# Retention heads 1 to 3: values and gate in seven quarter products, weighted values by tokens

## The chip, the cores and the metric

The kernel runs on one core of one Trainium2 chip. The metric is the device time of one execution in microseconds (us); lower is better. TensorE multiplies, VectorE and ScalarE do the element work, GpSimd (POOL) some of it, and SyncE (SP) issues the loads.

## What is computed

A trunk of two layers over 512 tokens of width 1024, all in float32: retention, FFN, RG-LRU, FFN, with norms before and after each. The change is in the retention layer:

```python
proj = x @ w_in                      # x: normed, 512 x 1024
q, k, v, g = jnp.split(proj, ...)    # 4 heads: q, k 256 wide, v, g 512 wide
q = rope(q); k = rope(k) * (DK ** -0.5)
scores = (q @ k.T) * decay           # causal, decay by head
o = scores @ v                       # the reference does it in chunks of 128
oc = o - o.mean(-1)
o = oc * lax.rsqrt(mean(oc * oc) + EPS)
return (o * silu(g)) @ w_out
```

## The kernel before

**Products.** Every float32 operand is split into a high part in fp32r (a cast on ScalarE, L163) and the rest as a low part (a subtraction on VectorE, L165). A product is then a triple, `mm3` (L291 to L293): high by high, high by low, low by high, three matmuls into the same PSUM bank. `Pre` makes the parts of the normed input (the norm's factor for a token is multiplied in later: `pre0.cols` holds it by tokens, `pre0.rb` spread over partitions).

**Heads.** The loop over four heads stands in `trunk` behind `rope`. For a head it forms the values by tokens (`pv`, four token tiles, weights in four chunks), centers them (`center`), then the queries and keys by features (`group`, two tiles each) with their rotation, the first half of the gate (`gate(0)`), the scores in four tiles that keep only the causal columns (512, 384, 256, 256 wide), `gate(1)`, and the weighted values by features: for each of four feature tiles the four score tiles are taken through (L291 to L293, `pav`). As tokens then lie along the free axis, the norm over a head's 512 features needs TensorE twice: `rchain` sums the squares with a vector of ones (L364, `st_gn`), takes the root in small instructions on VectorE (L374 to L381), and spreads it with diagonal matrices (L394, `rb_gn`). The products of the gate with the norm's factor and the `Silu` stand at L771 and L773. The results are split again (`Hr`) for the output projection `ro`, in four groups of two tiles over 16 tiles of features.

**FFN.** The FFN's up projection is made by blocks already: `Corners` holds four quarters of the normed input (token half by odd or even feature tile) and four sums of them, `Form` makes the sums of weight quarters `t1` to `t4` (L187), and seven products stand for eight. `LEFT`, `WEIGHTS` and `LATER_PAIR` name which sum meets which, `turn` (L860) transposes the results.

**What sets the order.** Each engine runs its instructions in the order written, which a planner lays out: `later` keeps a clock that `mm3` moves on by 0.4224 ns a column (`NS_PER_COL`), and a step given to `later.after(ns, ...)` is written when that clock is due. `later.until(cond)` writes waiting steps at once until the condition holds. `order` lists the weight items; `advance` splits items ahead of their use (five of the plain ones, 12 us of products of the `Form` ones, eight at most held), and `load_ahead` issues loads four ahead on SP. SBUF is a pool of 50 slots of 128x1024 (`SLOTS`), PSUM has six banks for sums (`acc`) and two others (`aux`).

## Time and profile before

| | us |
|---|---|
| median of 3 runs | 1385.68 (1385.38 to 1386.33) |
| profiled execution | 1384.3 |
| its span, first to last instruction | 1382.4 |
| TensorE busy in it | 1346.6 |
| VectorE busy in it | 900.6 |
| ScalarE busy in it | 665.4 |

The profile lists one execution, engine by engine. A busy time of TensorE counts any moment with a matmul in flight; matmuls overlap, so how long one takes in a row of them is read from the distance of their starts. The first product of head 1 starts at 86.65 us, heads 2 and 3 follow 78.8 us apart, and the output projection starts behind head 3.

### The profile page before, as it was taken

How to read it: one execution, taken by the hardware profiler on the slowest of the kernel's cores; microseconds unless marked ns; L12 is line 12 of the kernel's file. 1: busy time of each engine (PE TensorE's matmuls, PEld its weight loads, DVE VectorE, ACT ScalarE, POOL GpSimd, SP SyncE). 2: the span in 40 equal slices, each digit the busy share in tenths (PEclk: the TensorE clock that was granted, in tenths of full speed). 3: DMA queues.
4: the chain of work that ended last, by engine and by line, in shares of the span. 5: the costliest groups of instructions: out<-in, count | busy, mean ns of one | idle time of the engine just before them, and what ended most of it. 6: DMA issues, size and time to landing. Idle time of an engine off the chain costs nothing.

```text
span 1382.4 us, 17330 instructions
## 1 busy us (share of the span) xinstructions
PE 1346.6 (97%) x6760; PEld 1144.8 (83%) x6760; DVE 900.6 (65%) x1320; ACT 665.4 (48%) x983; POOL 117.6 (9%) x129
## 2 busy tenths in 40 slices
PE   8999999999999899999999999999997999999996
PEld 6888888888897678888889998888986888888886
DVE  7755455567337988787521787788579987775313
ACT  5423333334435665546422537787465555564311
POOL 1000000000015300000000710000052000000001
PEclk9999999999999999999999999999999999999998
DMA  8232312223343223233432543224333233323311
GB/s 332 76 102 62 115 63 85 77 76 112 102 141 119 93 92 94 89 122 101 119 100 78 169 136 105 78 77 153 122 108 121 78 106 122 113 89 103 92 61 62
DMA packets 48914, 146.77 MB, mean 106 GB/s; under 512 B 5472, under 2 KB 13792, under 8 KB 48832
## 3 DMA queue, kind: packets, MB, share of 16 engines
q1 hardware_dynamic: 45072, 135.16, 30.0%
q0 software_dynamic: 2608, 9.45, 2.0%
q8 instruction: 53, 0.87, 0.3%
q10 hardware_dynamic: 1152, 1.05, 0.2%
q14 instruction: 29, 0.24, 0.1%
HBM read 137.25 MB, written 8.39 MB: 105 GB/s over the span
## 4 chain that ended last, share of the span: by engine, by line
PE 54%; DVE 3%; POOL 1%; issue 1%; ACT 1%; DMA 0%; POOLq 0%; ACTq 0%; DVEq 0%
PE ps_fo L291 6%; PE ps_fo L292 6%; PE ps_fo L293 6%; PE b L291 3%; PE b L293 3%; PE b L292 3%; PE c L291 2%; PE c L293 2%; PE c L292 2%; PE a L292 2%; PE a L293 2%; PE a L291 2%; PE ps_y L291 1%; PE ps_y L293 1%; PE ps_y L292 1%; PE ps_lo L291 1%
## 5 line engine op out<-in xcount | busy, mean ns | idle before, releaser
L291 PE MATMUL ps_fo<-hh,wh_fo 128*128 128x512 f32 (+1 forms) x440 | 153.2, 348 | 0.0
L292 PE MATMUL ps_fo<-hl,wh_fo 128*128 128x512 f32 (+1 forms) x440 | 152.5, 347 | 0.0
L293 PE MATMUL ps_fo<-hh,wl_fo 128*128 128x512 f32 (+1 forms) x440 | 152.5, 347 | 0.0
L165 DVE TENSOR_TENSOR wl_s_t<-t,wh_s_t 128x1024 fp32r<-128x1024 f32 x80 | 98.0, 1248 | 21.7 <-ACT wh_s_t L163 21.7
L165 DVE TENSOR_TENSOR wl_s_b<-wr,wh_s_b 128x1024 fp32r<-128x1024 f32 x60 | 74.1, 1238 | 32.1 <-ACT wh_s_b L163 32.1
L291 PEld LDWEIGHTS ps_fo<-hh,wh_fo 128*128 128x128 f32 x440 | 83.3, 189 | 10.3
L293 PEld LDWEIGHTS ps_fo<-hh,wl_fo 128*128 128x128 f32 x440 | 83.3, 189 | 10.3
L292 PEld LDWEIGHTS ps_fo<-hl,wh_fo 128*128 128x128 f32 x440 | 83.3, 189 | 10.2
L163 ACT CAST wh_s_t<-t 128x1024 fp32r<-128x1024 f32 x80 | 80.6, 1051 | 15.9 <-DVE t L187 15.6
L163 ACT CAST wh_s_b<-wr 128x1024 fp32r<-128x1024 f32 x60 | 61.0, 1061 | 3.3 <-DVE wl_s_t L165 3.3
L861 ACT COPY hf<-turn 128x512 f32<-128x512 f32 x40 | 21.5, 590 | 79.6 <-PE turn L860 79.6
L165 DVE TENSOR_TENSOR wl_fo<-wr,wh_fo 128x1024 fp32r<-128x1024 f32 (+1 forms) x48 | 51.8, 1131 | 7.9 <-ACT wh_fo L163 7.9
L187 DVE TENSOR_TENSOR t<-wr,wr 128x1024 f32<-128x1024 f32 x40 | 50.4, 1260 | 0.0
L187 DVE TENSOR_TENSOR t<-t,wr 128x1024 f32<-128x1024 f32 x40 | 48.8, 1220 | 0.2
L163 ACT CAST wh_fo<-wr 128x1024 fp32r<-128x1024 f32 (+1 forms) x48 | 43.9, 984 | 0.0
L165 DVE TENSOR_TENSOR wl_g<-wr,wh_g 128x1024 fp32r<-128x1024 f32 x16 | 19.5, 1223 | 35.0 <-ACT wh_g L163 34.9
L431 POOL TENSOR_TENSOR pssq_f<-pssq_f,psq_f 128x256 f32<-128x256 f32 x28 | 35.7, 1285 | 35.1 <-ACT psq_f L430 34.2
L773 ACT ACTIVATE sg<-sg 128x512 f32<-128x512 f32 x16 | 10.1, 632 | 58.9 <-DVE sg L771 58.9
L771 DVE TENSOR_TENSOR sg<-ps_g,rb_r 128x512 f32<-128x512 f32 x16 | 11.1, 692 | 41.3 <-PE ps_g L293 41.3
L291 PE MATMUL b<-wh_s_t,Xf_s3h 128*128 128x512 f32 x80 | 32.2, 403 | 5.7 <-ACT u L956 5.7
L752 ACT ACTIVATE vs<-pv,y_prer 128x512 f32<-128x512 f32 x16 | 11.0, 690 | 53.7 <-PE pv L293 53.7
L293 PE MATMUL c<-wh_s_t,Xf_s1l 128*128 128x512 f32 x80 | 31.9, 399 | 4.4 <-DVE Xf_s1l L492 4.4
(1222 smaller groups left out, 4047.0 us busy)
## 6 DMA issues: line engine op xcount, KB each, us to landing
wr<-in_w_s SPq DMA_DIRECT2D x80, 512.0 KB, 3.9
wr<-in_w_fo SPq DMA_DIRECT2D x40, 512.0 KB, 3.6
wr<-in_w_li SPq DMA_DIRECT2D x24, 512.0 KB, 4.1
wr<-in_w_g SPq DMA_DIRECT2D x16, 512.0 KB, 4.0
wr<-in_w_ro SPq DMA_DIRECT2D x16, 512.0 KB, 3.8
wr<-in_w_v SPq DMA_DIRECT2D x13, 512.0 KB, 3.9
wr<-in_w_lo SPq DMA_DIRECT2D x12, 512.0 KB, 3.8
wr<-in_w_q SPq DMA_DIRECT2D x8, 512.0 KB, 3.7
```

Source lines behind the costliest of these rows:

```text
L163: act.copy(hi[:, :c], raw[:, :c])
L165: dve.tensor_tensor(lo[:, :c], raw[:, :c], hi[:, :c].bitcast(F32), op=ALU.subtract)
L187: dve.tensor_tensor(q[f, e], x, y, op=ALU.add)
L291: pe.matmul(out, lhsT=lh, rhs=rh, start=bool(first), stop=False, skip_group_check=chained)
L292: pe.matmul(out, lhsT=lh, rhs=rl, start=False, stop=False, skip_group_check=chained)
L293: pe.matmul(out, lhsT=ll, rhs=rh, start=False, stop=bool(last), skip_group_check=chained)
L431: eng.tensor_tensor(self.ssq[:, a:b], self.ssq[:, a:b], sq[:, a:b], op=ALU.add)
L752: act.activation(vs[i], pv[i], AF.Copy, scale=pre0.cols[i], accum_out=sm[:, i:i + 1])
L771: dve.tensor_tensor(gr, ps, rb, op=ALU.mult)
L773: later.after(700 * (m + 1), lambda gr=gr: act.activation(gr, gr, AF.Silu))
L861: act.copy(put(m), ps.rearrange("p (m t) -> p m t", m=2))
```

## The change

Head 0 keeps its values and gate as full products, but both now by tokens (`flat`). In heads 1 to 3 values and gate are one product of the normed input with a 1024 by 1024 matrix, made as in the FFN from quarters: rows are token halves, the inner halves are even and odd feature tiles, columns are values and gate. `Whole` forms the four sums of input quarters once, in head 0; `pair_planner` plans the 14 weight items of a head; `head_pair` runs the seven products p1, p5, p2, p6, p3, p7, p4 in six banks and writes the scores between p7 and p4 (`inner`). The weighted values are formed by tokens (`attend`), from score tiles as the fixed operand and values as the moving one, and only for the causal tiles; their square is summed by ScalarE's accumulator (`accum_out`), the root is taken by `root` straight from it, gate and root are multiplied in by VectorE, and the result is transposed in four groups of four (`finish_head`, `turned`). `attend` of a head is written behind the next head's queries; that of head 3 by `later.after(W_AV, ...)` inside the output projection. The diff's core (`root`, `center`, `scores` and `product` hold code that was inline before; `plan_ffn` and the FFN call the shared functions and do the same as before):

```diff
+W_GN_H = 6500
+W_TURN_H = 1500
+W_AV = 4500
+W_HR0 = 0
+W_HR = 1000
...
+    def root(sums, n, name, quick=False):
...
+        return y
...
-            m = sp.tile([P, 4], F32, tag="m", name=f"m_{name}_{a}")[:, :nt]
...
+            y = root(ps[:, :nt], n, f"{name}_{a}", quick)
...
+    LEFT = {"p1": (0, 0), "p2": (0, 1), "p3": "s4", "p4": (1, 1), "p5": "s1", "p6": "s2", "p7": "s3"}
+    class Whole(Pre):
+        def __init__(self, gi, name):
+            super().__init__(gi, name)
+            self.forms = {}
+        def sums(self, xs):
+            full = [[slot(f"X{self.name}f{c}{q}") for c in range(2)] for q in range(2)]
+            s = {f: slot(f"X{self.name}_{f}") for f in ("s1", "s2")}
+            def whole(j):
+                act.activation(full[j % 2][j // 4][:, j % 4 // 2 * S:][:, :S], xs[j], AF.Copy, scale=ng[:, self.gi, j:j + 1])
+            def add(f, x, y, op):
+                if f not in s:
+                    s[f] = slot(f"X{self.name}_{f}")
+                for c in range(2):
+                    dve.tensor_tensor(view(s[f][:, c * S:(c + 1) * S]), part(x, c), part(y, c), op=op)
+            def view(z):
+                return z.rearrange("p (i t) -> p i t", i=2)
+            def part(x, c):
+                if isinstance(x, str):
+                    return view(s[x][:, c * S:(c + 1) * S])
+                return view(full[x[1]][c])[:, :, x[0] * 256:(x[0] + 1) * 256]
+            def two(f):
+                hi, lo = slot(f"X{self.name}_{f}h", F32R), slot(f"X{self.name}_{f}l", F32R)
+                act.copy(hi, s[f])
+                def low():
+                    dve.tensor_tensor(lo, s[f], hi.bitcast(F32), op=ALU.subtract)
+                    self.forms[f] = hi, lo
+                later.after(1500, low)
+            steps = []
+            for j in range(KD):
+                steps += [lambda j=j: whole(j), 1500]
+            by = {z[0]: z for z in Corners.SUMS}
+            for f in ("s1", "s2", "s4", "s3"):
+                steps += [lambda f=f: add(*by[f]), 2500, lambda f=f: two(f), 2500]
+            later.seq(*steps[:-1])
+        def left(self, q, i, p):
+            if isinstance(q, tuple):
+                at = q[0] * 256 + p * P
+                return [z[:, at:at + P] for z in self.tiles[2 * i + q[1]]]
+            later.until(lambda: q in self.forms)
+            return [z[:, i * 256 + p * P:][:, :P] for z in self.forms[q]]
+    def product(key, r, banks, first, pre, done=None):
+        for e in range(2):
+            with Chunk("s", *key, WEIGHTS[r], e) as w:
+                for p in range(2):
+                    for i in range(2):
+                        x = pre.left(LEFT[r], 2 * e + i, p)
+                        mm3(banks[p], x, [z[:, i * S:(i + 1) * S] for z in w], first and not e + i, e + i == 2, True)
+                    if e and done:
+                        done(p)
...
+    HEAD_PAIR = ("p1", "p5", "p2", "p6", "p3", "p7", "p4")
+    head_form = pair_planner("v", t["w_vg"], 0)
+    for h in range(HEADS):
+        if not h:
+            plan_flat("v0", [t["w_v"][:, 2 * c:2 * c + 2].rearrange("p k m -> p (k m)") for c in range(4)])
+        plan(f"q{h}", t["w_q"][h], KD)
+        plan(f"k{h}", t["w_k"][h], KD)
+        if not h:
+            plan_flat("g0", [t["w_g"][:, 2 * c:2 * c + 2].rearrange("p k m -> p (k m)") for c in range(4)])
+        else:
+            for r in HEAD_PAIR:
+                for e in range(2):
+                    head_form(h, r, e)
...
-    pre0 = Pre(0, "r")
+    pre0 = Whole(0, "r")
...
+    def center(h, at, ps, V, apart=False):
+        n = len(ps)
+        vs = [big(f"vs{h}_{at + i}", kind="vs") for i in range(n)]
+        sm = sp.tile([P, 4], F32, tag="sm", name=f"sm{h}_{at}")[:, :n]
+        nm = sp.tile([P, 4], F32, tag="nm", name=f"nm{h}_{at}")[:, :n]
+        vh = []
...
+        def fill(i):
+            act.activation(vs[i], ps[i], AF.Copy, scale=pre0.cols[at + i], accum_out=sm[:, i:i + 1])
+        def finish():
+            later.seq(lambda: None, 700 * n, mean, 1500, low)
+        if apart:
+            return fill, finish
+        for i in range(n):
+            fill(i)
+        finish()
...
+    def head_pair(h, V, sg, inner):
+        A, C, B = ([acc(f"{z}v{h}_{p}") for p in range(2)] for z in "acb")
+        u, five = ([big(f"{z}{h}_{p}", kind=z) for p in range(2)] for z in ("u2v", "p5v"))
+        def silu(g, i):
+            sg[i] = g
+            later.after(800, lambda: act.activation(g, g, AF.Silu, scale=pre0.cols[i]))
+        def seed(p):
+            act.copy(B[p], A[p])
+        def p6(p):
+            act.copy(u[p], B[p])
+        def p5(p):
+            act.copy(five[p], C[p])
+        def p3(p):
+            dve.tensor_tensor(u[p], C[p], u[p], op=ALU.subtract)
+            silu(u[p], p)
+        def p7(p):
+            dve.tensor_tensor(five[p], five[p], B[p], op=ALU.subtract)
+            silu(five[p], 2 + p)
+        fill, finish = center(h, 2, B, V, True)
+        for r, banks, first, done in (("p1", A, True, seed), ("p5", C, True, p5), ("p2", A, False, None), ("p6", B, False, p6),
+                                      ("p3", C, False, p3), ("p7", B, False, p7), ("p4", B, False, fill)):
+            if r == "p4":
+                inner()
+            product(("v", h), r, banks, first, pre0, done)
+            if r == "p2":
+                later.after(100, lambda: center(h, 0, A, V))
+        finish()
+    def finish_head(h, ps, sg, ssq):
+        og = [big(f"og{h}_{i}", kind="og") for i in range(4)]
+        def scaled():
+            y = root(ssq, 512, f"gn{h}")
             for i in range(4):
+                dve.scalar_tensor_tensor(out=og[i], in0=ps[i], scalar=y[:, i:i + 1], in1=sg[i], op0=ALU.mult, op1=ALU.mult)
+        def turned(m):
+            pt = aux(f"turn_r{h}_{m}")
+            for i in range(4):
+                pe.transpose(pt[:, i * P:(i + 1) * P], og[i][:, m * P:(m + 1) * P], ident)
+            hr = big(f"hr{h}_{m}", kind="hr")
+            act.copy(hr, pt)
+            if h < HEADS - 1:
+                raw[4 * h + m] = hr
+            else:
+                split(hr, f"Hr{4 * h + m}", lambda z: Hr.__setitem__(4 * h + m, z))
+            if m < 3:
+                later.after(W_TURN_H, lambda: turned(m + 1))
+        later.seq(lambda: None, 1000, scaled, W_GN_H, lambda: turned(0))
...
+    def attend(h, V, Sc, sg):
+        ssq = sp.tile([P, 4], F32, tag="os", name=f"os{h}")
+        po = []
+        for i in range(4):
+            later.until(lambda: None not in V[:i + 1] + Sc[:i + 1])
+            po.append(acc(f"pav{h}_{i}"))
+            for kk in range(i + 1):
+                hi, lo, q0, _ = Sc[kk]
+                at = i * P - q0
+                mm3(po[i], (hi[:, at:at + P], lo[:, at:at + P]), V[kk], kk == 0, kk == i)
+            sq = big(f"osq{h}_{i}", kind="osq")
+            act.activation(sq, po[i], AF.Square, accum_out=ssq[:, i:i + 1])
+        finish_head(h, po, sg, ssq)
+    decs, before = [dec0], None
+    for h in range(HEADS):
+        if h:
+            decs.append(slot(f"dec_{h}")[:, :640])
+            pool.dma_start(decs[h], t["decay"][h])
+        q, k, V, sg, Sc = [None, None], [None, None], [None] * 4, [None] * 4, [None] * 4
+        if not h:
+            pv = flat("v0")
+        psq = group(f"q{h}", X)
+        if not h:
+            later.until(lambda: pre0.scaled)
+            center(0, 0, pv, V)
+            dve.tensor_tensor(cosr, cos_raw, pre0.rb, op=ALU.mult)
+            dve.tensor_tensor(sinr, sin_raw, pre0.rb, op=ALU.mult)
+            pre0.sums(x0)
+        rope(psq, f"q{h}", q.__setitem__)
+        if h:
+            attend(*before)
+        rope(group(f"k{h}", X), f"k{h}", k.__setitem__)
+        if h:
+            def inner():
+                scores(h, q, k, Sc)
+                if h == HEADS - 1:
+                    for i in range(12):
+                        later.after(W_HR0 + W_HR * i, lambda i=i: split(raw[i], f"Hr{i}", lambda z: Hr.__setitem__(i, z)))
+            head_pair(h, V, sg, inner)
+        else:
+            gate0 = lambda i, ps: act.activation(sg[i], ps, AF.Silu, scale=pre0.cols[i])
+            sg = [big(f"sg0_{i}", kind="sg") for i in range(4)]
+            flat("g0", gate0)
+            scores(0, q, k, Sc)
+        before = h, V, Sc, sg
+    later.after(W_AV, lambda: attend(*before))
...
+    vg = wi[:, 2048:].reshape(2, 2, 2, P, 2, HEADS, 512).transpose(5, 2, 4, 0, 3, 1, 6)
...
-        "w_v": _tiles(wi[:, 2048:4096], 4),
-        "w_g": _tiles(wi[:, 4096:], 8),
+        "w_v": _tiles(wi[:, 2048:2560], 1)[0],
+        "w_g": _tiles(wi[:, 4096:4608], 1)[0],
+        "w_vg": vg.reshape(HEADS * 8, P, 1024),
```

## Rows read from the trace of the kernel before

**Rows 1.** Page: busy times, a costly group, a load (last number: us to landing).

```profile
PE 1346.6 (97%) x6760; PEld 1144.8 (83%) x6760; DVE 900.6 (65%) x1320; ACT 665.4 (48%) x983; POOL 117.6 (9%) x129
...
L861 ACT COPY hf<-turn 128x512 f32<-128x512 f32 x40 | 21.5, 590 | 79.6 <-PE turn L860 79.6
...
wr<-in_w_s SPq DMA_DIRECT2D x80, 512.0 KB, 3.9
```

**Rows 2.** Stretches: busy us of PE, PEld, DVE, ACT, POOL; clock; DMA; GB/s.

```profile
20.00:400.00 380.00, 380.00 (x1838) 322.14 (x1837) 213.29 (x354) 138.03 (x208) 3.63 (x5) 1.00 0.29 96
86.65:165.42 78.77, 78.77 (x378) 66.68 (x377) 42.96 (x74) 26.16 (x40) 0.54 (x1) 1.00 0.26 85
440.00:500.00 60.00, 52.41 (x229) 41.89 (x228) 58.65 (x78) 33.50 (x49) 14.94 (x10) 0.97 0.29 105
500.00:680.00 180.00, 179.36 (x829) 148.84 (x828) 135.67 (x153) 100.70 (x131) 0.00 (x0) 1.00 0.34 106
```

**Rows 3.** Waits of TensorE, whole span: us in total, times, longest.

```profile
PE b L291 <- ACT u L956: 5.7, 1, 5.7
PE c L293 <- DVE Xf_s1l L492: 4.4, 2, 2.5
```

**Rows 4.** Timeline of TensorE, output projection: start us, us, engine, line.

```profile
339.70 0.39 PE L293 MATMUL ps_ro<-Hr10h,wl_ro 128*128 128x512 f32 x1
...
345.82 0.39 PE L293 MATMUL ps_ro<-Hr15h,wl_ro 128*128 128x512 f32 x1
```

**Rows 5.** Timeline of TensorE, weighted values of head 0 and what follows.

```profile
78.94 0.39 PE L291 MATMUL pav<-s_0h,v_0h 128*128 128x512 f32 x1
...
86.65 0.39 PE L291 MATMUL pv<-wh_v,Xr_0h 128*128 128x512 f32 x1
```

**Rows 6.** Timeline of TensorE around the two norm groups of head 0.

```profile
89.85 0.39 PE L293 MATMUL pv<-wh_v,Xr_0h 128*128 128x512 f32 x1
90.08 0.95 PE L364 MATMUL st_gn<-ones_sq,ossq 128*128 128x1 f32 x8
...
91.21 0.40 PE L292 MATMUL pv<-wl_v,Xr_1h 128*128 128x512 f32 x1
...
94.20 0.39 PE L293 MATMUL pv<-wh_v,Xr_3h 128*128 128x512 f32 x1
...
95.56 0.39 PE L292 MATMUL pv<-wl_v,Xr_2h 128*128 128x512 f32 x1
```

**Rows 7.** Timeline of TensorE around four transposes, first FFN.

```profile
505.36 0.39 PE L293 MATMUL a<-wh_s_b,Xf_01l 128*128 128x512 f32 x1
505.59 0.60 PE L860 MATMUL turn<-ident,hr 128*128 128x128 f32 x4
...
506.26 0.40 PE L292 MATMUL a<-wl_s_b,Xf_01h 128*128 128x512 f32 x1
```

**Rows 8.** One tile, 500 to 680 us: ns min/median/max, first, last.

```profile
L860 PE MATMUL turn<-ident,h x40: 270/272/329, 500.6 to 662.5; 128*128 128x128 f32 x40
```

**Rows 9.** Groups of VectorE in head 1's period: busy us, mean ns.

```profile
L165 DVE TENSOR_TENSOR wl_g<-wr,wh_g 128x1024 fp32r<-128x1024 f32 x4 | 4.9, 1223 | 10.9 <-ACT wh_g L163 10.9
...
L771 DVE TENSOR_TENSOR sg<-ps_g,rb_r 128x512 f32<-128x512 f32 x4 | 2.8, 692 | 10.3 <-PE ps_g L293 10.3
...
L748 DVE SCALAR_TENSOR_TENSOR v_0l<-vs,nm,v_0h 128x512 fp32r<-128x512 f32 x2 | 1.4, 747 | 0.9 <-ACT v_0h L743 0.9
```

**Rows 10.** Groups of VectorE, 500 to 680 us: sums of weight quarters.

```profile
L187 DVE TENSOR_TENSOR t<-wr,wr 128x1024 f32<-128x1024 f32 x14 | 17.1, 1218 | 0.0
```

**Rows 11.** Groups of ScalarE in head 1's period.

```profile
L163 ACT CAST wh_g<-wr 128x1024 fp32r<-128x1024 f32 x4 | 4.1, 1042 | 0.0
L752 ACT ACTIVATE vs<-pv,y_prer 128x512 f32<-128x512 f32 x4 | 2.8, 690 | 17.9 <-PE pv L293 17.9
```

**Rows 12.** Timeline of VectorE, the root in head 0's norm.

```profile
91.06 0.16 DVE L374 TENSOR_SCALAR m_gn<-st_gn 128x4 f32<-128x4 f32 x1 [2.29 <-PE st_gn L364]
...
93.25 0.16 DVE L381 SCALAR_TENSOR_TENSOR y_gn<-tm_gn,y_gn 128x4 f32<-128x4 f32 x1
```

More of the change, by code (lines that the diff above doesn't have):

```diff
@@ L596, in out_proj @@
             finish(a, b)
-    for h in range(HEADS):
-        plan_flat(f"v{h}", [t["w_v"][h][:, 2 * c:2 * c + 2].rearrange("p k m -> p (k m)") for c in range(4)])
-        plan(f"q{h}", t["w_q"][h], KD)
-        plan(f"k{h}", t["w_k"][h], KD)
-        for g in range(2):
-            plan(f"g{h}_{g}", t["w_g"][2 * h + g], KD)
     def plan_joint(names, ws, K, uses):
@@ L755, in trunk @@
-        if h:
-            center(pv, V, h)
-        psq = group(f"q{h}", X)
-        if not h:
-            later.until(lambda: pre0.scaled)
-            center(pv, V, h)
-            dve.tensor_tensor(cosr, cos_raw, pre0.rb, op=ALU.mult)
-            dve.tensor_tensor(sinr, sin_raw, pre0.rb, op=ALU.mult)
-        rb = pre0.rb
-        rope(psq, f"q{h}", q.__setitem__)
-        rope(group(f"k{h}", X), f"k{h}", k.__setitem__)
-        sg = []
-        def gate(g, h=h, sg=sg):
-            for m, ps in enumerate(group(f"g{h}_{g}", X)):
-                gr = big(f"sg{h}_{2 * g + m}", kind="sg")
-                dve.tensor_tensor(gr, ps, rb, op=ALU.mult)
-                sg.append(gr)
-                later.after(700 * (m + 1), lambda gr=gr: act.activation(gr, gr, AF.Silu))
@@ L775, in trunk @@
-        gate(0)
-        later.until(lambda: None not in q + k)
-        Sc = [None] * 4
+                        mm3(ps[i], [z[:, i * P:(i + 1) * P] for z in X[kt]],
+                            [z[:, kk * S:(kk + 1) * S] for z in (hi, lo)], kt == 0, kt == KD - 1)
+                    if done and c == 3:
+                        done(i, ps[i])
+        return ps
+    def head_pair(h, V, sg, inner):
[25 more added lines that the diff above has]
+        finish()
@@ L778, in trunk, with scores @@
+    def scores(h, q, k, Sc):
+        dec = decs[h]
         sh = [big(f"s{h}_{i}h", F32R, "s") for i in range(3)]
@@ L801, in trunk @@
             weigh()
-        gate(1)
-        if h == HEADS - 1:
-            for i in range(12):
-                later.after(1200 * i, lambda i=i: split(Hr[i], f"Hr{i}", lambda z: Hr.__setitem__(i, z)))
-        later.until(lambda: None not in V + Sc)
-        og = [big(f"og{h}_{e}", kind="og") for e in range(4)]
-        ssq = big(f"ossq{h}", kind="osq")
-        for e in range(4):
-            ps = acc(f"pav{h}_{e}")
-            for i in range(4):
-                hi, lo, q0, n = Sc[i]
-                mm3(ps[:, q0:], (V[i][0][:, e * P:(e + 1) * P], V[i][1][:, e * P:(e + 1) * P]), (hi, lo), i == 0, i == 3)
-            if e == 0:
-                act.square(ssq, ps)
-            else:
-                sq = big(f"osq{h}_{e}", kind="osq")
-                act.square(sq, ps)
-            dve.tensor_tensor(og[e], ps, sg[e], op=ALU.mult)
-            if e:
-                dve.tensor_tensor(ssq, ssq, sq, op=ALU.add)
@@ L823, in then @@
-        def then(pr, _, og=og, h=h):
-            for e in range(4):
-                i = 4 * h + e
-                dve.tensor_tensor(og[e], og[e], pr, op=ALU.mult)
-                if h < HEADS - 1:
-                    Hr[i] = og[e]
-                else:
-                    split(og[e], f"Hr{i}", lambda z, i=i: Hr.__setitem__(i, z))
-        rchain(ssq, 0, S, 512, f"gn{h}", then, W_GN)
+    def attend(h, V, Sc, sg):
[11 more added lines that the diff above has]
+        finish_head(h, po, sg, ssq)
@@ L842, in ffn @@
         A, B, C = ([acc(f"{z}{layer}_{p}") for p in range(2)] for z in "abc")
-        LEFT = {"p1": (0, 0), "p2": (0, 1), "p3": "s4", "p4": (1, 1), "p5": "s1", "p6": "s2", "p7": "s3"}
-        def product(j, r, banks, first):
-            for e in range(2):
-                with Chunk("s", layer, j, WEIGHTS[r], e) as w:
-                    for p in range(2):
-                        for i in range(2):
-                            x = pre.left(LEFT[r], 2 * e + i, p)
-                            mm3(banks[p], x, [z[:, i * S:(i + 1) * S] for z in w], first and not e + i, e + i == 2, True)
         def turn(hs, put):
@@ L991, in run @@
                 to[j] = tiles(j)
-            product(j, r, BANK[r], r in ("p1", "p5"))
+            product((layer, j), r, BANK[r], r in ("p1", "p5"), pre)
             later.after(300, lambda: pair(j, r, to[j]))
```

106 lines of the change are left out of this document (49 added, 57 removed).

## Prediction

> **What bounds the kernel now.** I read the page's busy times first, then the stretches, then the waits, then single instructions of TensorE. TensorE is busy for 97% of the span [rows 1]. More to the point, from 20 to 400 us, which holds all four retention heads after their start, it is busy for 380.00 of 380 us at a granted clock of 1.00, so its full level of 2.4 GHz, while VectorE has 213.29 us of work there [rows 2]. The stage is bound by the number of products, and no wait of TensorE is left in it. So an edit that only removes a wait earns nothing in this stage, and an edit that removes products earns each of them in full, as long as the vector engines can feed the rest. The waits of TensorE that the profile lists lie outside: the two largest after the start are those on `u` and on `Xf_s1l`, a half evicted and a part of a token sum [rows 3], in the openings of the FFNs. In the first of these, 440 to 500 us, VectorE is busy for 58.65 of 60 us and TensorE for only 52.41 [rows 2]: that is what quarter products look like when their sums are made too late; from 500 to 680 us the same quarter products run with VectorE at 135.67 of 180 us and TensorE at 179.36 [rows 2].
>
> **The unit.** In the output projection 27 steps from 339.70 to 345.82 us [rows 4] make 0.2267 us from one 128x512 product to the next. The recorded duration, 0.39, overlaps the next one and is not used. A head takes 78.77 us: from 86.65 [rows 5] to 165.42, the stretch in [rows 2]. Check: 288 products of values, queries, keys and gate give 65.3, the weighted values 7.71, the two norm groups 1.81 (both below), which leaves 3.9 for the scores and next to nothing for waiting.
>
> **1. Values and gate in seven quarter products, heads 1 to 3.** Before: 4 chunks x 4 token tiles x 2 = 32 triples for the values, 32 for the gate, 192 products. After: 7 quarter products x 2 halves of K x 2 x 2 = 56 triples, 168 products, each 512 columns wide. 24 fewer x 0.2267 = 5.44 us a head, 16.3 us for three.
>
> **2. Weighted values by tokens, all four heads.** Before: four rows of tiles from 78.94 to 86.65 us [rows 5], 7.71 us. After: tile i needs only score tiles 0 to i, so 1+2+3+4 = 10 triples = 30 products x 0.2267 = 6.80. That saves 0.91 a head, 3.6 in all.
>
> **3. The norm over the head's values.** It becomes an accumulated square of ScalarE and no longer goes over TensorE. Removed are the group of eight small products for the sums, which stretches three starts from 2 x 0.2267 to 1.36 us (89.85 to 91.21, so 0.91), and the group that spreads the root (94.20 to 95.56, 0.91) [rows 6]. 1.81 a head, 7.3 in all.
>
> **4. The transposes that this costs.** The result now lies by tokens and must be turned: 16 per head, in four groups of four. The FFN has just such a group: 505.36 to 506.26 us with four transposes between [rows 7], 0.90 less 0.45 = 0.45 us a group. 16 groups: +7.2. The record gives 270 ns for each [rows 8], but as with the products it overlaps its neighbours.
> The Trainium skill (TensorE: Matmul & The Clock Gate, Part 4: PE-mode transpose) gives a transpose about 275 ns in a kernel. By that price 64 of them would be an estimate of 17.6 us instead of 7.2. The duration of the record agrees with it, the spacing of the starts doesn't, and I take the spacing.
>
> **Sum of TensorE's work:** -16.3 - 3.6 - 7.3 + 7.2 = -20.0 us.
>
> **5. What VectorE and ScalarE get for it.** Per head 14 weight splits instead of 8 (6 x 1.22 us [rows 9]), eight sums of weight quarters (8 x 1.22 [rows 10]) and four subtractions (4 x 0.69) are added; four gate products, four products with the root and three sums of squares (11 x 0.69 [rows 9]) go. The head's 42.96 us of VectorE [rows 2] become 43 + 7.3 + 9.8 + 2.8 - 7.6 = 55.3 of now 72.4 us, or 76%. In 500 to 680 us the share is 75%, and the loss was 0.6 in 180 us. ScalarE gets six casts of 1.04 [rows 11], six evictions and four copies of turned tiles (10 x 0.59 [rows 1]): 26.16 + 12.1 = 38 of 72.4. So I cost both at nothing. The cover is the lead of the splits, 12 us of products ahead; if it is gone, see the first rival. In head 0 the token sums (8 copies on ScalarE, then eight half adds of 0.69 and four splits of 1.22, some 10.5 us of VectorE) lie behind the key and gate products, 33 us, and are needed only after scores, queries, weighted values and keys, 32 us later. Cost nothing; at worst some of those 10.5 us. The loads stay at 4 MB a head on SP's queue, in smaller steps; the decay load stays first on POOL's queue and meets nothing new.
>
> **6. What is moved.** Scores go between the products p7 and p4, weighted values of head h behind head h+1's queries, those of head 3 into the output projection. No wait stood at their old places, so this gains nothing. It can cost, in two places.
> (a) The first turn of each head stands 1000 + 6500 ns of planned products behind the weighted values, and the plan counts 216 ns for a product that takes 227, so 7.9 us. Its chain: the square of the last tile as the values' eviction with its sum (0.69 [rows 11], with the read behind it and the start taken as 1.2), the root's 13 small instructions (91.06 to 93.41, 2.4 us) [rows 12], four scaled products of at most 0.75 [rows 9], 6.6 in all. That leaves 1.3 us of slack, from which a split or a sum queued ahead on VectorE takes 1.22. Behind the waiting transpose stand the key products, on TensorE's one queue. Bounds: 0 and, with two sums and two splits ahead, 4.9 - 1.3 = 3.6 a head. A gain is excluded, as nothing waits there now. I take 0.3 for each of three heads, near the lower end, since turns of 500 to 680 us waited little: 1.0.
> (b) In the output projection the fourth turn of head 3 is planned 12.0 us behind the weighted values, and the first product on its result (`Hr15`) at 15.6 + 3 x 0.65 - 4.5 = 13.0. Its chain is 0.45 of transposes, 0.59 for the copy [rows 1], as much for the high part and 0.69 for the low one, 2.3 us, where 1.1 + 0.2 are there: 1.0 missing. Behind it stands the rest of the projection on TensorE. Bounds: 0, and 3.3 with a weight cast of 1.04 [rows 11] ahead on ScalarE and a split of 1.22 on VectorE. I take 1.3, near the bare chain.
>
> **Result.** -20.0 + 1.0 + 1.3 = -17.7 us. The profiled execution took 1384.3 us (span 1382.4), so 1366.6; the median of the runs is 1385.68, 0.1% above it, so **1368 us**.
>
> **The rivals.**
> *VectorE fills up in the pair.* In a pair's own stretch (168 products and the scores, 42 us) the sums crowd: 27 us of splits and sums, the rotation of the keys, the subtractions and the weighing of scores come to some 35 to 41 us, between the 75% and the 98% of the two FFN stretches. At the loss of 440 to 500 us, 7.6 in 60 [rows 2], three pairs lose 3 x 42 x 0.127 = 16 us: 1384. At half of it 1376. For it: ScalarE's evictions and VectorE's subtractions stand in the same queues as the splits, and `b <- u` was such a wait. Against: POOL, which was busy in that stretch (14.94 us), is idle in the heads [rows 2], and the first splits are made ahead, behind the key products.
> *Slots run short and the pair's first quarters come late: slower.* The token sums hold eight more of 50 slots through the heads, a pair opens with four loads at once, and SP issues in order. If they can only start when the pair does, each pair opens with 3.9 us to land [rows 1], 1.04 for the cast [rows 11], 1.22 for the sum that stands between cast and split and 1.22 for the split [rows 9, 10]: 7.4, for three pairs 22: 1390. It decides from 17.7 / 3 = 5.9 us a pair. Against: the FFN runs with 16 slots of token parts and the same loads.
> *Turns cost the clock: slower.* If a series of four turns had the products around it granted 1.2 GHz, the 3 x 1.6 + 4 x 0.45 = 6.6 us that a series covers would take twice that; four series make 26 us: 1394. It decides from 4.4 us a series. Against: 500 to 680 us holds the 40 transposes of `h` [rows 8] and more, at a clock of 1.00 [rows 2]. The Trainium skill (same page and section) says that a transpose "doesn't count as PE-busy the same way"; by that rule the level could fall, and the trace shows no fall where they are strewn among products.
> *The transposes cost their full 0.27 us.* 64 x 0.27 = 17.3, 10 more: 1378. Against it speaks the one group read above.
>
> **How the numbers follow.** Forecast 0.71 (1363 to 1374), VectorE full 0.18, slots 0.05, clock 0.03, full transposes 0.03. The range runs from 1363.5 (no waits, and 2 us less in the first FFN, whose 7.6 us of gaps may shift either way) up to 1379, which takes in the lower half of the first rival and the last one; it leaves out about 0.17. A measurement tells 0.2%, 2.8 us, from no change. Faster: 0.71 + 0.14 + 0.03 = 0.88; the same: 0.04, the first rival's upper end; slower: 0.08.
>
> **What would show it.** Right: each of heads 1 to 3 about 72.4 us from query to query, TensorE busy throughout at a clock of 1.00, VectorE near 75%, no norm products with `gn` on TensorE, transposes of `og` in fours that push two starts apart by 0.45. Step 6 right: short waits of `turn_r` on `og`, and one of the output projection on `Hr15`. Wrong: waits of TensorE on `wl_v`, `wh_v`, on sums of quarters, or on `five`/`u` (first rival); SP waiting up to a pair's start (second); a granted clock under 1 between 90 and 320 us (third); starts 0.27 apart in a turn (last). If the period is as forecast and the total is not, the loss is behind 320 us, where nothing was meant to change.

## The result, and the profile after

The changed kernel takes **1368.1 us** (median; 1367.9 to 1368.4) where the kernel before takes 1386.0 beside it: a ratio of **0.987 (0.985 to 0.989)**. The forecast was 1368. The profiled execution took 1367.93 us, 16.4 us less than that of before; its span is 1366.2, 16.2 less.

The busy times of the page of after, which answer to [rows 1]:

```profile
PE 1331.9 (97%) x6616; PEld 1127.5 (83%) x6616; DVE 935.1 (68%) x1329; ACT 711.5 (52%) x1063; POOL 117.3 (9%) x129
```

The share of TensorE has not moved; the work under it has become less. The stretches of after, beside [rows 2] (us, then busy time and instructions of PE, PEld, DVE, ACT, POOL, then the granted clock, DMA share and GB/s). The first is the whole stage; the second, fourth and fifth are heads 1 to 3 from query to query; the third is head 1's pair alone, from the first product of p1 to the last of p4:

```profile
20.00:400.00 380.00, 377.65 (x1824) 317.71 (x1823) 257.71 (x392) 190.67 (x303) 12.26 (x15) 1.00 0.33 106
79.62:152.08 72.46, 72.46 (x336) 60.39 (x335) 52.92 (x78) 35.85 (x58) 0.54 (x1) 1.00 0.30 92
109.16:152.08 42.92, 42.92 (x201) 35.94 (x200) 33.21 (x40) 27.35 (x41) 0.54 (x1) 1.00 0.27 82
152.08:224.52 72.44, 72.44 (x336) 60.38 (x335) 53.67 (x77) 37.59 (x61) 0.54 (x1) 1.00 0.28 92
224.52:296.95 72.43, 72.43 (x336) 60.38 (x334) 55.89 (x81) 39.62 (x65) 0.00 (x0) 1.00 0.30 95
```

A head takes 72.44 us instead of 78.77, TensorE fills all of it at a clock of 1.00, and VectorE has 53 to 56 us in it. All waits of TensorE before 400 us (total, times, longest):

```profile
PE ps_v L296 <- ACT Xr_0h L424: 5.9, 1, 5.9
PE c L298 <- DVE Xf_00l L548: 1.2, 1, 1.2
PE ps_ro L297 <- DVE Hr15h L350: 1.2, 1, 1.2
```

The first is the start of the kernel and the second the opening of the first FFN. The third is the only one in the changed code.

**Where the time went.** The first product of the first FFN's down projection (`ps_fo`) is a mark behind everything that was changed. Its group of instructions in before and after (the fourth figure from the left, behind the durations, is the start of the first, then that of the last):

```profile
L291 PE MATMUL ps_fo<-hh,wh_fo x440: 277/389/476, 645.3 to 1370.0; 128*128 128x512 f32 x88, 128*128 128x256 f32 x59
```

```profile
L296 PE MATMUL ps_fo<-hh,wh_fo x440: 277/389/476, 627.7 to 1352.9; 128*128 128x512 f32 x88, 128*128 128x256 f32 x59
```

17.6 us are gained at the mark and 17.1 are left at the last product, so the later stages give back 0.5; another 0.9 goes in the last microseconds of the span. At the mark the account is: -20.0 of products, as forecast, +1.43 for the wait on `Hr15h`, +0.27 for a gap in head 3's weighted values, +0.7 in the first 84 products, which are the same code in both (21.73 us instead of 21.00): -17.6. The 1.43 is counted from start to start (326.33 to 328.21 us, less two products; the lines stand below); the profile's 1.15 runs only from the recorded end of the product ahead, which overlaps the next one. The 0.7 is not a longer wait, as the first product starts at 5.94 us in both: the first products stand some 0.43 us apart in both, and the spacing falls to 0.23 at 9.5 us in before and at 10.5 in after.

### The profile page after: what moved, and what is told of

Its sections match the earlier page's. It is cut to its first block, busy times and chain, and to the rows that moved or that the text cites. A ratio compares the mean times of both kernels' runs of the same rounds, so it can differ in the third digit from the quotient of the medians.

```text
span 1366.2 us, 17146 instructions
## 1 busy us (share of the span) xinstructions
PE 1331.9 (97%) x6616; PEld 1127.5 (83%) x6616; DVE 935.1 (68%) x1329; ACT 711.5 (52%) x1063; POOL 117.3 (9%) x129
## 4 chain that ended last, share of the span: by engine, by line
PE 55%; DVE 3%; issue 1%; POOL 1%; ACT 1%; POOLq 0%; DVEq 0%; ACTq 0%
PE ps_fo L296 6%; PE ps_fo L298 6%; PE ps_fo L297 6%; PE b L296 3%; PE b L297 3%; PE b L298 3%; PE c L296 2%; PE c L298 2%; PE c L297 2%; PE a L297 2%; PE a L298 2%; PE a L296 2%; PE ps_y L296 1%; PE ps_y L297 1%; PE ps_y L298 1%; PE ps_lo L296 1%
## 5 line engine op out<-in xcount | busy, mean ns | idle before, releaser
L296 PEld LDWEIGHTS ps_fo<-hh,wh_fo 128*128 128x128 f32 x440 | 83.3, 189 | 10.2
L168 ACT CAST wh_s_t<-t 128x1024 fp32r<-128x1024 f32 x80 | 80.7, 1052 | 15.9 <-DVE t L192 15.6
L442 POOL TENSOR_TENSOR pssq_f<-pssq_f,psq_f 128x256 f32<-128x256 f32 x28 | 35.4, 1272 | 35.5 <-ACT psq_f L441 34.6
L170 DVE TENSOR_TENSOR wl_s_v_t<-t_v,wh_s_v_t 128x1024 fp32r<-128x1024 f32 x24 | 28.9, 1222 | 9.7 <-ACT wh_s_v_t L168 9.7
L296 PE MATMUL c<-wh_s_b,Xf_s4h 128*128 128x512 f32 x80 | 32.2, 402 | 2.0 <-ACT p L1107 2.0
L1123 ACT ACTIVATE h<-b,y_pref 128x512 f32<-128x512 f32 x20 | 13.7, 690 | 38.2 <-PE b L298 38.2
L298 PE MATMUL c<-wh_s_b,Xf_s4l 128*128 128x512 f32 x80 | 31.7, 397 | 0.7 <-DVE Xf_s4l L569 0.7
```

What stands on the lines that cost most here:

```text
L168: act.copy(hi[:, :c], raw[:, :c])
L170: dve.tensor_tensor(lo[:, :c], raw[:, :c], hi[:, :c].bitcast(F32), op=ALU.subtract)
L296: pe.matmul(out, lhsT=lh, rhs=rh, start=bool(first), stop=False, skip_group_check=chained)
L298: pe.matmul(out, lhsT=ll, rhs=rh, start=False, stop=bool(last), skip_group_check=chained)
L442: eng.tensor_tensor(self.ssq[:, a:b], self.ssq[:, a:b], sq[:, a:b], op=ALU.add)
L1123: act.activation(g[p], B[p], AF.Silu, scale=pre.cols[2 + p])
```

## The experiments

Eleven kernels, each the kernel after with the edit shown. "Above after" compares medians with 1368.1. The kernel before, run beside each group of them, had medians of 1386.0 to 1386.6, so such a difference holds to about 0.6 us. The start adds to that: the first 84 products have the same code in all of these kernels but the last two, and the 85th starts at 27.7 us in the profiled execution of after but between 28.4 and 30.1 in theirs. A cleaner measure is the time from that product to the mark above, the first `ps_fo`: 600.0 us in after and 618.3 in before.

### One part undone or repeated

**Full products again in heads 1 to 3** (`e1_flat_all`): values and gate by tokens as in head 0, no sums of the input and no quarter products. Of the terms of the sum it undoes step 1 alone; with it the order changes, as values then stand ahead of the queries and the scores behind the gate.

```diff
-        if not h:
-            pv = flat("v0")
+        pv = flat(f"v{h}")
+        if h:
+            center(h, 0, pv, V)
...
-            pre0.sums(x0)
...
-            head_pair(h, V, sg, inner)
+        flat(f"g{h}", gate0)
+        scores(h, q, k, Sc)
```

> Undoes step 1 alone: values and gate of heads 1 to 3 are full products by tokens, as in head 0, with the weighted values by tokens, the norm and the transposes kept; scores stand behind the gate, no token sums. Theory (the number of products sets the time): 72 products x 0.2267 = 16.3 us slower than the changed kernel, 1384.4, which leaves a gain of about 1.6 us on the kernel before (3.6 + 7.3 - 7.2 of steps 2 to 4, less waits); a period of 72.4 + 5.44 = 77.9 us a head. Rival (the gain comes from what was moved, not from the products): under 8 us slower than the changed kernel, 1376 or less.

Measured: 1387.06 us, ratio 1.001 (1.000 to 1.002), 19.0 above after. Head 1 in the stretches, and then the waits of TensorE before 400 us:

```profile
81.01:158.89 77.88, 77.88 (x361) 64.88 (x360) 35.15 (x60) 28.60 (x48) 0.54 (x1) 1.00 0.26 79
```

```profile
PE ps_v L296 <- ACT Xr_0h L424: 7.0, 1, 7.0
PE turn_r L897 <- DVE og L892: 1.6, 4, 0.7
PE ps_ro L297 <- DVE Hr0h L350: 1.1, 1, 1.1
PE ps_ro L296 <- ACT Hr0h L347: 1.0, 1, 1.0
```

The period is 77.88 us, 5.42 above the 72.46 of after: the 24 products at 0.2267, 5.44. That is 16.3 for three heads. The 2.7 above it are not the products: the start waited 1.1 longer, and without p4 behind the scores head 3's end has no cover, so its turns and `Hr0` are waited for. From the 85th product to the mark it takes 19.7 more than after: 16.3 of products, and 3.4 of those waits, less the one on `Hr15h`, which is gone here. So the quarter products are worth what was forecast. With them undone the kernel is level with before: the other steps gain 3.7 by their sum, and the three waits behind the heads come to 3.7 as well.

**Each transpose twice** (`e2_turn_twice`):

```diff
-            for i in range(4):
+            for i in (0, 1, 2, 3, 0, 1, 2, 3):
                 pe.transpose(pt[:, i * P:(i + 1) * P], og[i][:, m * P:(m + 1) * P], ident)
```

> Every group of four transposes is issued twice into the same bank, 64 more transposes. Theory (spacing of starts): 16 groups x 0.35 to 0.45 = 5.6 to 7.2 us slower than the changed kernel, 1373.7 to 1375.3, at a granted clock of 1.00 in the heads. Rival (each costs its recorded 0.27 us): 17.3 slower, 1385.4. Rival (transposes cost the clock): a granted clock under 1 in the heads and over 20 us more.

Measured: 1374.29 us, 0.992 (0.990 to 0.993), 6.2 above after. TensorE in order of time (start, duration, then the instruction) around one turn, first in after, then here; and last the stretch from 20 to 400 us here:

```profile
105.26 0.39 PE L298 MATMUL ps_k<-Xr_7h,wl_k 128*128 128x512 f32 x1
105.50 0.60 PE L903 MATMUL turn_r<-ident,og 128*128 128x128 f32 x4
105.85 0.48 PE L296 MATMUL ps_k<-Xr_4h,wh_k 128*128 128x512 f32 x1
106.16 0.40 PE L297 MATMUL ps_k<-Xr_4h,wh_k 128*128 128x512 f32 x1
```

```profile
107.47 0.39 PE L298 MATMUL ps_k<-Xr_7h,wl_k 128*128 128x512 f32 x1
107.70 1.03 PE L903 MATMUL turn_r<-ident,og 128*128 128x128 f32 x8
108.49 0.48 PE L296 MATMUL ps_k<-Xr_4h,wh_k 128*128 128x512 f32 x1
```

```profile
20.00:400.00 380.00, 378.82 (x1844) 319.45 (x1843) 250.65 (x375) 187.17 (x294) 7.28 (x9) 1.00 0.31 100
```

In after, 105.26 to 106.16 is 0.90, less two products 0.45: the price that was taken. The turn pushes the next product off by 0.35 us with four transposes and by 0.79 with eight, so one more costs 0.11. 64 more cost 6.2 us by the medians, 6.7 by the time from the 85th product to the mark and 7.0 by the spacing, and not 17.3. The clock stays at 1.00 with twice the transposes, so the clock rival falls with the full price.

**The norm's two groups of small products back** (`e3_norm_groups`), with constants as their operands and nobody reading the results, so only TensorE's own time returns:

```diff
+        def sums():
+            st = aux(f"st_gn{h}")
+            for i in range(4):
+                pe.matmul(st[:, i:i + 1], lhsT=ones_sq, rhs=ones_sq[:, 0:1], start=True, stop=True)
...
+        later.after(2000, sums)
+        later.after(4500, spread)
```

> Gives the two norm groups of the kernel before (four sums with a vector of ones, four spreading products) back to each head, as dead work on constants that waits for nothing and that nothing waits for. Theory (step 3): 4 x 1.81 = 7.3 us slower than the changed kernel, 1375.4. Rival (they are hidden in gaps of TensorE): under 2 us.

Measured: 1375.65 us, 0.992 (0.991 to 0.994), 7.5 above after, and 7.3 from the 85th product to the mark. Step 3 said 7.3. Nothing of the old norm's price was a wait: removing the products alone is the gain.

### The wait on Hr15h

In after, the last turn of head 3 and its results, in order of time on ScalarE, then VectorE, then TensorE:

```profile
323.76 0.59 ACT L905 COPY hr<-turn_r 128x512 f32<-128x512 f32 x1 [0.59 <-PE turn_r L903]
324.38 0.62 ACT L347 CAST Hr15h<-hr 128x512 fp32r<-128x512 f32 x1
324.91 1.05 ACT L168 CAST wh_ro<-wr 128x1024 fp32r<-128x1024 f32 x1
...
325.99 1.23 DVE L170 TENSOR_TENSOR wl_ro<-wr,wh_ro 128x1024 fp32r<-128x1024 f32 x1 [2.10 <-ACT wh_ro L168]
327.13 0.68 DVE L350 TENSOR_TENSOR Hr15h<-hr,Hr15h 128x512 fp32r<-128x512 f32 x1
...
326.33 0.39 PE L296 MATMUL ps_ro<-Hr15h,wh_ro 128*128 128x512 f32 x1
327.87 0.50 PE L297 MATMUL ps_ro<-Hr15h,wh_ro 128*128 128x512 f32 x1 [1.15 <-DVE Hr15h L350]
328.21 0.40 PE L298 MATMUL ps_ro<-Hr15h,wl_ro 128*128 128x512 f32 x1
```

The high part is ready at 325.00 and VectorE is idle, but the next instruction in its queue is the split of a projection weight, whose cast ends at 325.96. Only behind it comes the low part, and TensorE stands for 1.15 us. **The low part placed first** (`e4_low_first`) tells the two readings apart, a chain that is too long or a queue in the wrong order:

```diff
-                split(hr, f"Hr{4 * h + m}", lambda z: Hr.__setitem__(4 * h + m, z))
+                split(hr, f"Hr{4 * h + m}", lambda z: Hr.__setitem__(4 * h + m, z), 0)
```

> The low parts of head 3's four turned tiles are written right behind their high parts, ahead of any weight split that falls due in the 1.2 us between. Theory now (the wait of the output projection on Hr15 comes from a weight split queued ahead of it on VectorE): the wait of 1.15 us is gone, about 1 us faster than the changed kernel. Rival, as predicted (the bare chain from transpose to low part is too long): the wait stays at 0.8 us or more.

Measured: **1365.83 us**, 0.985 (0.984 to 0.987), 2.3 below after. The waits of TensorE up to 420 us and VectorE in order of time:

```profile
PE ps_v L296 <- ACT Xr_0h L424: 6.3, 1, 6.3
PE c L298 <- DVE Xf_00l L548: 1.2, 1, 1.2
```

```profile
325.79 0.69 DVE L350 TENSOR_TENSOR Hr15h<-hr,Hr15h 128x512 fp32r<-128x512 f32 x1 [1.14 <-ACT Hr15h L347]
326.75 1.22 DVE L170 TENSOR_TENSOR wl_ro<-wr,wh_ro 128x1024 fp32r<-128x1024 f32 x1 [0.26 <-ACT wh_ro L168]
```

The wait is gone; the weight split now stands behind the low part, and nobody waits for it. The chain was short enough; the queue was not in order. The stretch from the last turn to the end of the projection became 1.45 us shorter, which is the whole of that wait from start to start; 0.3 of it is lost again before the mark. So about 0.9 of the medians' difference is not shown to come from the edit. In the profiled executions it isn't the start, which came 0.7 later here: it lies behind the mark, where the code is the same (0.5 between the first and the last `ps_fo`, 0.8 behind that). The intervals of the two ratios overlap, but the wait is gone in the trace, and all runs of this version (1365.3 to 1367.1) lie below all of after's (1367.9 to 1368.4): it has the lowest median of the kernels here.

### VectorE: how much room was there?

**Each sum of weight quarters made twice, then three times** (`e5_sums_twice`, `e6_sums_thrice`), for the heads' weights alone. The added work is 8 x 1.22 us a head, the values stay the same.

```diff
-                dve.tensor_tensor(q[f, e], x, y, op=ALU.add)
+                for _ in range(2 if self.key[1] == "v" else 1):
+                    dve.tensor_tensor(q[f, e], x, y, op=ALU.add)
```

> Each sum of weight quarters of heads 1 to 3 is written twice: 8 x 1.22 = 9.8 us more of VectorE a head, 53 to 56 us of 72.4 become 63 to 66 (89%), and in a pair's stretch 35.0 of 44.75 come near 44.8. Theory (step 5: VectorE's share is hidden as long as it stays under the period, since splits lead by 12 us): within 2 us of the changed kernel, period 72.4 to 73. Rival (VectorE fills up in the pair, at the loss of the first FFN, 12.7% of 3 x 42 us): 16 us slower, waits of TensorE on wl_s_v.

Measured: 1377.96 us, 0.994 (0.993 to 0.996), 9.9 above after; my theory had allowed 2. Head 2, and some of the waits of TensorE from 20 to 400 us:

```profile
155.33:230.04 74.71, 73.73 (x336) 60.12 (x334) 63.01 (x86) 37.27 (x60) 0.54 (x1) 1.00 0.26 85
```

```profile
PE pav L298 <- DVE v_2l L827: 1.6, 1, 1.6
PE av L298 <- DVE wl_s_v_b L170: 1.5, 3, 0.5
...
PE ps_ro L298 <- DVE Hr0h L351: 1.1, 1, 1.1
```

The period grows by 2.27 us a head although VectorE has 63.0 of 74.7 us, 84%. That is 7.0 for the three heads; the rest comes behind them, where head 3's weighted values and the projection's first tile (`v_2l`, `Hr0h`) are now waited for.

> Each of these sums is written three times: 19.5 us more of VectorE a head, 73 to 75 us for a period of 72.4. Theory: now VectorE is the bound, the period becomes 75 to 80 us, 8 to 23 us slower than the changed kernel, with waits of TensorE on wl_s_v or on what VectorE subtracts. If it is within 3 us, VectorE's share is not what the first rival hangs on.

Measured: 1407.16 us, 1.016 (1.014 to 1.017), 39 above after; the expectation ended at 23. The same stretch of head 2, and the largest wait:

```profile
164.71:249.08 84.37, 77.36 (x336) 61.95 (x334) 72.69 (x95) 37.43 (x60) 0.54 (x1) 0.96 0.24 79
```

```profile
PE cv L298 <- DVE wl_s_v_t L170: 10.8, 3, 3.6
```

At 86% of the period VectorE costs 11.9 us a head, 36 of the 39, and the rest is again lost behind the heads. A share of the head is therefore the wrong measure. The whole pair is not the right one either: the expectation of `e5_sums_twice` took its 35.0 of 44.75 us from a stretch that begins 1.8 us too early, inside the key products (107.33 to 152.08). The pair itself has 33.2 of 42.9, and with the sums made twice VectorE still stands idle for 5.4 of the pair's 45.2 us in head 2. What is full is the first part of the pair. The products p1, p5, p2 and p6 of head 2 in after, with the sums twice, and three times:

```profile
181.59:204.32 22.73, 22.73 (x106) 18.81 (x105) 19.29 (x21) 15.95 (x24) 0.00 (x0) 1.00 0.14 48
```

```profile
184.84:208.41 23.57, 23.06 (x105) 18.64 (x104) 23.43 (x25) 12.40 (x19) 0.00 (x0) 1.00 0.15 52
```

```profile
194.22:224.98 30.76, 26.06 (x105) 20.63 (x104) 30.42 (x30) 12.56 (x19) 0.00 (x0) 0.89 0.15 52
```

VectorE has 3.4 us of room there in after and 0.1 to 0.3 in the other two. With the sums twice this part grows by 0.84 us and the products behind it by 1.43; VectorE has its first gap only at 211.0 us, 2.6 us into them. Three times, it grows by 8.0 and the rest by 3.9. That the first four products set the limit is read from these three traces; no run moved work out of them alone.

**A shorter lead** (`e7_short_lead`): the splits of the heads' weights start 5.4 us of products ahead, not 12.

```diff
+LEAD_V = 5441
...
-            if j > i and (least or (ns >= (LEAD_E if z.early else LEAD_S) if z.early or isinstance(z, Form) else j > i + AHEAD)):
+            if j > i and (least or (ns >= (LEAD_E if z.early else LEAD_V if z.key[1] == "v" else LEAD_S) if z.early or isinstance(z, Form) else j > i + AHEAD)):
```

> The weight items of heads 1 to 3 are split two items ahead (5.44 us of planned products) instead of 12 us ahead. Theory (the lead is the cover): an item is then written some 3.6 us ahead of its use and its chain of cast, sum and split takes 1.04 + 1.22 + 1.22 = 3.5, so any queue ahead shows: 3 to 15 us slower than the changed kernel, waits on wl_s_v. If nothing changes, the cover is smaller than named and 3.6 us are enough.

Measured: 1377.98 us, 0.994 (0.993 to 0.996), 9.9 above after. The waits:

```profile
PE av L297 <- ACT wh_s_v_b L169: 2.8, 3, 0.9
PE av L298 <- DVE wl_s_v_b L171: 2.3, 3, 0.8
```

The heads lose 8.7 us, and 8.3 of it lies in the opening of the pair, in the products p1 (`av`), which take 8.6, 8.7 and 10.2 us instead of 6.4; the later products of the pair are fed almost in time even with the short lead (0.15 us a head lost in p3). The waits come to 5.1 as the profile counts them, from the recorded end of the product ahead; from start to start they cost more, and in head 3 the granted clock of p1 is 0.83, where it is 1.00 in heads 1 and 2. So the lead is the cover, as the prediction said, but almost only of the opening. Once the pair runs, what counts is VectorE's room in it.

**Fewer slots** (`e8_slots45`): 45 instead of 50.

```diff
-SLOTS = 50
+SLOTS = 45
```

> 45 slots in SBUF instead of 50, for the whole program. Theory (slots don't bind in the heads): heads 1 to 3 keep a period of 72.4 us; the total is within 3 us of the changed kernel unless the FFNs lose. Rival (slots are short): loads of a pair's first quarters start late, each pair opens with a wait on wh_s_v or wl_s_v, 3 us a head or more.

Measured: 1372.41 us, 0.990 (0.989 to 0.992), 4.3 above after. Head 2:

```profile
152.96:225.40 72.44, 72.44 (x336) 60.38 (x334) 53.89 (x77) 37.84 (x61) 0.00 (x0) 1.00 0.27 86
```

The head is the same to 0.01 us. The 4.3 us are lost behind the heads: from the 85th product the mark comes 4.4 later, 3.7 of which are lost between the heads and the first FFN. So the slots rival had five slots of room in the heads, and it falls.

### The turns' slack

**The turns 3 us earlier** (`e10_turn_early`):

```diff
-W_GN_H = 6500
+W_GN_H = 3500
```

> The first turn of a head is written 1000 + 3500 ns of planned products behind the weighted values instead of 1000 + 6500, so 4.7 us of real ones. Theory (step 6a, with the chain of 6.05 us that the changed kernel's trace shows): each head's first transposes wait about 1.3 us for og, 4 x 1.3 = 5 us slower than the changed kernel, 1373. If it is within 1 us, the chain is shorter than read; over 10 us, more than the chain waits.

Measured: 1373.21 us, 0.991 (0.989 to 0.992), 5.1 above after, as expected, and 4.4 from the 85th product to the mark. The one wait of TensorE between 20 and 400 us that it adds:

```profile
PE turn_r L903 <- DVE og L898: 3.8, 10, 1.0
```

In after there is none. Head 1 of after, in order of time: the first products behind the weighted values, the root's first instruction on VectorE, the last two scaled products, and the turn:

```profile
169.76 0.39 PE L296 MATMUL ps_k<-Xr_0h,wh_k 128*128 128x512 f32 x1
...
170.68 0.17 DVE L373 TENSOR_SCALAR m_gn<-os 128x4 f32<-128x4 f32 x1 [1.55 <-ACT osq L954]
...
174.41 1.40 DVE L898 SCALAR_TENSOR_TENSOR og<-pav,y_gn,p5v 128x512 f32<-128x512 f32 x2
...
177.93 0.60 PE L903 MATMUL turn_r<-ident,og 128*128 128x128 f32 x4
```

The chain takes 169.76 to 175.81, 6.05 us, and the turn comes 8.17 behind: 2.1 us of slack. Taking away 3 us leaves 0.9 missing, and the turns wait up to 1.0.

### Quarter products in head 0 too

**Two attempts at a further gain** (`e9_head0_pair`, `e11_queries_first`), both with the edit of `e4_low_first`: head 0 also as a pair, so 24 products fewer. The sums of the input must then be made early. In the first, head 0's queries and keys open the kernel together and head 1's queries cover the sums; in the second all queries stand ahead of the first pair.

```diff
+    plan_joint(["q0", "k0"], [t["w_q"][0], t["w_k"][0]], KD, 1)
+    plan("q1", t["w_q"][1], KD)
+    plan_pair(0)
+    plan("k1", t["w_k"][1], KD)
+    plan_pair(1)
...
+    later.after(W_SUMS, lambda: pre0.sums(x0))
```

> Carries step 1 to head 0 too, with the low parts first as in e4_low_first: queries and keys of head 0 open the program together, then the queries of head 1, then head 0's pair; the keys of head 1 take head 0's weighted values between their two chunks; token sums begin 12 us into the program instead of behind the queries. Theory (products set the time): another 24 x 0.2267 = 5.4 us off, with the 1.2 of the other edit 1361 to 1362, no wait of TensorE from 20 to 300 us over 1 us. Rival (the token sums or the opening come late): waits on Xr_s1h or on the first weights, 3 to 6 us, 1365 to 1368.

Measured: 1378.24 us, 0.994 (0.993 to 0.996), 12.4 above `e4_low_first` instead of 5 below it. Two stretches and three waits:

```profile
20.00:30.00 10.00, 6.52 (x17) 4.55 (x16) 5.64 (x5) 6.14 (x9) 2.59 (x2) 0.67 1.02 396
...
60.00:70.00 10.00, 8.24 (x24) 6.26 (x25) 10.00 (x13) 6.10 (x8) 0.00 (x0) 0.66 0.15 52
```

```profile
PE ps_k L299 <- DVE wl_k L171: 3.2, 1, 3.2
PE cv L297 <- DVE q_a L804: 3.1, 1, 3.1
PE av L298 <- DVE wl_s_v_b L171: 2.4, 2, 2.1
```

The second kernel differs by the order of the queries; it also splits the opening's fourth weight item earlier, starts the sums of the input 2 us later, and puts the weighted values between the two chunks of the keys in heads 1 to 3:

```diff
-    plan("q1", t["w_q"][1], KD)
-    plan_pair(0)
-    plan("k1", t["w_k"][1], KD)
-    plan_pair(1)
+    for h in range(1, 4):
+        plan(f"q{h}", t["w_q"][h], KD)
```

> Head 0 in quarter products again, with what e9_head0_pair lost mended: the fourth weight item of the opening is split as soon as it lands, and the queries of all heads come before the first pair, so that VectorE has some 30 us more for the rotations and the token sums before it must make a pair's weight sums; keys of heads 1 to 3 take the weighted values of the head before between their two chunks. Theory (in e9 VectorE was full from 40 to 80 us and the opening waited for a split): both waits gone, 1361 to 1364. Rival (VectorE's total up to the end of head 0's pair is too much wherever it stands): waits on wl_s_v or Xr_s in head 0's pair stay, 1366 or more.

Measured: 1373.36 us, 0.991 (0.989 to 0.992), 7.5 above `e4_low_first`. One stretch and one wait:

```profile
80.00:90.00 10.00, 7.83 (x34) 5.84 (x33) 10.00 (x13) 3.19 (x5) 0.00 (x0) 1.00 0.23 76
```

```profile
PE ps_k L300 <- DVE wl_k L172: 3.7, 1, 3.7
```

Both expectations fell. Near the opening of head 0's pair VectorE is busy for 10.00 of 10 us: the sums of the input, the rotations and the weight splits meet there. The queries ahead moved that stretch from 60 to 80 us and made it cheaper, but did not empty it. The wait of over 3 us for a split of the key weights (`wl_k`), at 20 to 25 us, is the case of `Hr15h` again. In the first kernel the cast of these weights ends at 20.55, but the split starts at 23.32: ahead of it in VectorE's queue stand the additions of the norm's squares, from 17.47 on, the last of which waits 1.16 us for GpSimd's. The second kernel has the same order there, with the cast done at 20.49 and the split at 23.76. No run placed the split ahead of them. Head 0's full products are therefore not simply a gain left lying: with these orders they are the time in which VectorE makes the sums.

## Why the prediction was right

**Steps 1 to 4**, -20.0 us, hold term by term. Step 1: 77.88 against 72.46 a head when it is undone. Step 2: the weighted values run from 90.53 to 97.33 us in head 1, 6.80, as forecast against the 7.71 of [rows 5]; in head 3, inside the output projection, they take 7.07, because one product waits 0.12 us and the next ones start slower. That 0.27 was not foreseen. Step 3: 7.3 to 7.5 for 7.3. Step 4: 0.45 a group, and the one group of the FFN [rows 7] was a good enough base. The Trainium skill's price for a transpose (TensorE: Matmul & The Clock Gate, Part 4: PE-mode transpose), about 275 ns, agrees with the recorded duration here, 270 to 273 ns, but in a series each costs 110 ns. That the level of the clock could fall, by the rule of the same section of the Trainium skill, is not what these runs show: 1.00 in the stage with 64 transposes and with 128.

**Step 5** had the right number and too wide a margin. VectorE's 55.3 us a head came out as 52.9 to 55.9, and it cost nothing. But the reason given, a share of 76% like that of 500 to 680 us [rows 2], was not what protects it. The repeated sums show that 84% of the head already costs 2.27 us, and their traces show where the work crowds: in the first four products of the pair, in which VectorE had 3.4 us of room. The first rival looked at the pair, with 35 to 41 us of work in it. It came out at 33.2 to 35.5 in the three heads, about the lower end, and that is why the rival didn't happen. One further set of sums, 9.8 us a head, was enough to start the loss, 7 us in the heads instead of the rival's 16.

**Step 6a** was wrong in its size: 1.0 was taken for the turns and none was paid. Two terms erred to the same side: the chain took 6.05 us, not 6.6 (scaled products of 0.70 and a start of the root 0.92 behind the last product, not 1.2), and the turn came 8.17 behind, not 7.9. The earlier turns show that the chain is the right one.

**Step 6b** hit the size by another way: 1.3 taken, 1.43 paid from start to start (1.15 as the profile counts it). The step said that `Hr15` is needed 13.0 us behind the weighted values' place and the bare chain takes too long. In fact the first group of the projection goes through all tiles of features for two output tiles at once, so each tile of `Hr` lasts for two triples, 1.3 us, and `Hr15` is needed about 2 us later than was worked out (15.6 + 3 x 1.3 - 4.5 = 15.0). The bare chain would have been in time, as `e4_low_first` shows. What was late was the low part behind a weight split on VectorE, which the step had only as its upper bound.

**The sum**: -17.7 forecast, -17.6 at the mark behind the changed stage and -16.4 over the execution. So 1368 is in part errors that cancel: 1.0 for turns that was not paid, against 0.7 at the start, 0.27 in the weighted values and about 1.4 behind the mark. What is left of them, 1.3 in the profiled execution, was met by the 0.1% that the forecast added for the median: here the profiled execution is the median, to 0.2 us. That the total comes within 0.1 us of 1368 is luck; that the products leave in full is not.

**The rivals.** VectorE full in the pair: a real limit, but not reached. Slots: none missing in the heads even at 45. Clock and full transposes: shown false by the doubled transposes.

## What to carry to other kernels

Where the stretch, not only the kernel, has its engine full at a clock of 1.00, count the products that an edit takes away at their spacing: the gain comes in full as long as the engine that feeds them has room in that same stretch, and the room must be counted there, product by product, not over the period around it (here 84% of a head went with 99% of its fullest part, and cost 2.27 us). Cost an instruction by how far it pushes the next start, not by its recorded duration. Where the last small step of a chain meets a long weight split on the same queue, put the small step first; it took one argument here, removed a wait of 1.15 us and what came with it, 1.45 in all, and gave the lowest median, 1365.83 us.

## What was not expected of the hardware

- A transpose is recorded with 270 ns in any company, but eight in a row push the next product off by 0.79 us, four by 0.35: 0.11 each.
- A stall can cost more than its length. In `e6_sums_thrice` the granted clock of a head is 0.96, and in `e9_head0_pair` 0.67 and 0.66 in the two stretches above, in which TensorE was busy for 6.52 and 8.24 of 10 us: means of time at 2.4 and at 1.2 GHz. Not every stall does it: in `e11_queries_first` the stretch above has 7.83 of 10 us at 1.00, and in `e9_head0_pair` 50 to 60 us has 6.03 of 10 at 1.00, with the fall in the stretch behind it. Where TensorE never stood, in heads 1 to 3 of after, the clock was 1.00.
- The start of the kernel differs between executions with the same code there. The first product starts at 5.3 us in `e10_turn_early`, 5.9 in after, 7.0 in `e1_flat_all` and 7.4 in `e8_slots45`. The first products stand some 0.43 us apart, later ones 0.23, and the change comes between 9.5 us (before) and 14.6 (`e7_short_lead`). Together the 85th product starts between 26.9 (before) and 30.1 us (`e7_short_lead`), so up to 3 us of difference between two kernels' profiles can be that alone.
